# Layer 1 of a two-layer diffusion block: unsplit fp32 expert products for the first 32 blocks, and low parts kept on VectorE up to the expert loop

## Chip, cores and metric

The kernel runs on one core of one Trainium2 chip. The metric is the device time of one execution in microseconds (us), lower is better; for several runs the median is given.

## The reference

Two layers work on 256 latent tokens and 256 context tokens of width 1024. Each layer has an RMSNorm, one input projection, three attention mixers (A, B, W), a gated merge and an output projection; then a second RMSNorm and PEER, a layer of 128 x 128 = 16384 one-neuron experts of which every token picks 16 in each of 8 heads. The last layer computes the latent tokens only.

```python
def peer(h, w_pq, sub_keys, u_tab, v_tab):
    q = (hf @ w_pq).reshape(n, PEER_HEADS, 2, PEER_HALF)
    s = jnp.einsum('nhpd,hpkd->nhpk', q, sub_keys)
    ...
    top_s, pos = lax.top_k(cand_s, PEER_TOPK)
    g = jax.nn.softmax(top_s, axis=-1)
    ...
        a = jax.nn.gelu(jnp.einsum('cd,chkd->chk', hc, u), approximate=False)
        return jnp.einsum('chk,chkd->cd', gc * a, v)
```

For the latent tokens the kernel does not gather the picked experts. It computes all 16384 of them as dense products, 128 blocks of 128 experts, and multiplies each activation by a gate that is zero where the expert was not picked.

## The kernel before

Tokens lie along the free dimension, features along the 128 partitions. A matrix product with a weight comes in two forms.

- **Split** (`wsplit`, `mm3`, `mmw`; lines 292 to 294): a weight tile `raw` of 128 x 1024 is loaded, ScalarE (or VectorE) rounds each half of it to a high part `whi`, VectorE or GpSimd subtracts it to get a low part `wlo`, and TensorE runs three passes: high by high, high by low, low by high. The activation `h` is kept as a high and a low part as well.
- **Unsplit** (`mmd`, line 310): TensorE multiplies the fp32 tile `raw` by an fp32 activation (`h32`). Nothing else touches the weight.

`hmm` chooses between them: unsplit, if it is asked to and an fp32 activation was kept. Only `(layer 0, latent)` is in `DIRECT`, so in layer 1 there is none.

PEER of layer 1 runs in these steps, all recorded in program order by interleaved generators (`weave` gives each a share of the stretch) and then put on five in-order engine queues:

- `topk` (from line 946's scores): 16 query blocks `w_pq`, one product each, then the scores, then the best 16 keys of each half on VectorE (MAX8, FIND_INDEX8, MATCH_REPLACE8).
- `rank`: per 128 tokens the best 16 of 54 candidate pairs and their gates, on VectorE; three transposes on TensorE (line 1034) end it.
- `gbuild`: gate tables `gb` for 32 blocks. Per 16 tokens VectorE makes f16 one-hot tiles `t` (from `iot`), `oh` and `B`, TensorE multiplies them (line 1067, or line 1058 in the packed form of layer 1's loop). `B` has one buffer.
- `up(b)`: the first product of block b (`peer_u`) and its Gelu. Blocks 0 to 31 are computed ahead, in `dense_start`, from 45% of the gate work on, and kept in `gast`.
- `down(b)`: the second product (`peer_v`), in `dense`. In layer 0 (`PLAIN`) it is unsplit (line 1136); in layer 1 the gated activation `mt` is split into `pT` by ScalarE and VectorE, and the weight by `wsplit`. Beside blocks 0 to 31 the table for blocks 32 to 63 is built; from block 30 on `up(b + 2)` stands ahead of `down(b)`.

`lean` is a flag that `wsplit` reads: while it is set, every high part goes to ScalarE and every low part to VectorE. When it is off, `pick` sends each to the engine that its own load count says is free, and some of the low parts go to GpSimd. `norm_mod` and `gated` give some subtractions or additions to GpSimd too when it is off. It is cleared after layer 0's expert loop. Every VectorE, ScalarE and GpSimd instruction is recorded by one helper and shows as line 103.

Of the kernel before, what the change touches and what calls it, by code (L numbers as in the profile page):

```python
# [7 lines left out]
F32 = mybir.dt.float32  # L8
# [9 lines left out]
P = 128  # L18
T = 256
# [10 lines left out]
SW = (32, 32, 32, 32)  # L30
GR = 32
GSCALE = 32768.0
DIRECT = ((0, 0),)
K0, K1, K2 = 0.1, 0.5, 0.06
R0, R1, R2, R3 = 0.6, 0.30, 0.5, 0.9
PACKG = (1,)
# [2 lines left out]
PLAIN = (0,)  # L39
# [8 lines left out]
class Dummy:  # L48
# [5 lines left out]
    def __call__(self, *a, **k):  # L54
        return self

    def __getitem__(self, i):
        return self
# [8 lines left out]
class XView:  # L67


    def __init__(self, tiles):  # L70
        self.tiles = tiles

    def __call__(self, k):
        return self.tiles[k // 4][:, (k % 4) * T:(k % 4 + 1) * T]


class Engine:
# [30 lines left out]
class Net:  # L108
# [63 lines left out]
    def go(self, gen):  # L172
        for _ in gen:
            pass
# [527 lines left out]
    def attend(self, l, g, pre=False):  # L702

        lat = g == 0
        h, q, kv, kvt, f1, ms, ots = self.mx[g]
        kvs = [kv, self.kvc] if lat else [kv]
        m32 = (kvt[:, 0:2048] if lat else f1[:, 4096:6144]).rearrange("p (k t) -> p k t", k=KC)
        att = lambda nm, o: lambda n: n.attention(l, lat, nm, q, kvs, o)
        gq = lambda ch, nm: lambda n: n.gqa_q(l, lat, ch, nm, h, q)
        mb = lambda br, o: lambda n: n.merge_branch(l, br, h, o, m32, ms)  # L710

        def both(f1, f2):
            def run(n):
                yield from f1(n)
                yield from f2(n)
            return run

        if pre:
            yield from self.attention(l, lat, "a", q, kvs, ots[0])
            yield from self.weave(att("b", ots[1]), mb(0, ots[0]))  # L720
        else:
            yield from self.weave(att("a", ots[0]), gq(2, "b"))
            yield from self.weave(att("b", ots[1]), both(gq(3, "w"), mb(0, ots[0])))
        yield from self.weave(att("w", ots[0]), mb(1, ots[1]))
        yield from self.merge_branch(l, 2, h, ots[0], m32, ms)
        gth = self.small(f"gth{g}", [P, KC])
        self.V.tensor_scalar(gth, self.mods[l][:, 16:24, g], 0.5, None, OP.mult)
        xt = self.big.tile([P, 2, 4 * T], F32, tag="tk", name=self.nm("xt"))
        for n in range(2):
            self.nc.sync.dma_start(xt[:, n], self.xd[l, 0, g][n])  # L730
        x = XView([xt[:, n] for n in range(2)])
        ps = [self.psum(True) for _ in range(NTB)]
        for db in range(KC):
            w = self.wsplit(self.d["w_o"][l, db])
            po = self.psum()
            self.mmw(po[:, :T], w, ms[:, 0], ms[:, 1], KC)
            self.defer(lambda po=po, db=db: self.V.scalar_tensor_tensor(x(db), po[:, :T], gth[:, db:db + 1], x(db), OP.mult, OP.add))
            if db:
                self.sumsq(ps, x(db - 1), db - 1)
            yield 2.6  # L740
        self.flush()
        self.sumsq(ps, x(KC - 1), KC - 1)
        for n in range(2):
            self.nc.sync.dma_start(self.xd[l, 1, g][n], xt[:, n])
        htok = None
        if not lat:
            htok = [self.wk.tile([P, D], F32, tag=t, name=self.nm(t)) for t in ("ht", "gacc")]
        h32 = None
        if (l, g) in DIRECT:
            if g:  # L750
                h32 = self.big.tile([P, KC, T], F32, tag="h", bufs=2, name=self.nm("h32"))
            else:
                self.spare = self.gtile()
                h32 = self.spare[:, 0:KC, :]
        self.h32[g] = h32
        self.h2[g] = self.norm_mod(l, g, "g_ffn", 24, x, ps, htok, g == 0 or h32 is None, h32=h32)
        if not lat:
            self.ht = htok[0]
            self.nc.sync.dma_start(self.htok, htok[1])
        yield 1.0  # L760
# [164 lines left out]
    def topk(self, l, g, tok=False):  # L925


        V, S, PE, G = self.V, self.S, self.PE, self.G
        tk = self.big.tile([P, 2048], F32, tag="tk", name=self.nm("tk"))
        r4 = lambda a: a.rearrange("p (h s k) -> p h s k", h=H, s=2)  # L930
        s12 = [r4(tk[:, tb * 256:256 + tb * 256]) for tb in range(NTB)]
        i12 = [r4(tk[:, 512 + tb * 256:768 + tb * 256].bitcast(U32)) for tb in range(NTB)]

        def top16(vals, idx, src, tmp):
            V.max(vals[:, 0:8], src)
            V.max_index(idx[:, 0:8], vals[:, 0:8], src)
            V.match_replace(tmp, vals[:, 0:8], src, -3.0e38)
            V.max(vals[:, 8:16], tmp)
            V.max_index(idx[:, 8:16], vals[:, 8:16], tmp)

        qs = self.work("B", [P, 2, T])

        def score(hb, sk):
            ps = self.psum()
            for tb in range(NTB):
                PE.matmul(ps[:, tb * P:(tb + 1) * P], qs[:, hb % 2, tb * P:(tb + 1) * P], sk, start=True, stop=True)
            sc = self.work("t2", [P, NTB, P])
            S.activation(sc, ps[:, :T].rearrange("p (j e) -> p j e", e=P), AF.Copy)
            for tb in range(NTB):
                tmp = self.work("mt", [P, 256])  # L950
                top16(s12[tb][:, hb // 2, hb % 2, :], i12[tb][:, hb // 2, hb % 2, :], sc[:, tb, :], tmp[:, :P])

        sks = []
        for hb in range(16):
            sks.append(self.work("sk", [P, P]))
            self.nc.sync.dma_start(sks[-1], self.d["subk"][l, hb])
            pq = self.psum()
            self.hmm(pq[:, :T], self.d["w_pq"][l, hb], g)
            self.defer(lambda pq=pq, hb=hb: S.activation(qs[:, hb % 2, :], pq[:, :T], AF.Copy))
            if hb:  # L960
                score(hb - 1, sks.pop(0))
            yield 3.3
        self.flush()
        score(15, sks.pop())
        if tok:
            idx = self.wk.tile([P, NTB, P], U32, tag="gidx", name=self.nm("gidx"))
            gate = self.wk.tile([P, NTB, P], F32, tag="gate", name=self.nm("gate"))
            self.slot[g] = (idx, gate)
        else:
            self.slot[g] = self.big.tile([P, 4, T], F16, tag="slot", name=self.nm("slot"))  # L970
        self.tk = (tk, s12, i12, top16)
# [140 lines left out]
    def dense(self, l):  # L1112
# [12 lines left out]
        def down(b, gb, bi):  # L1125
            if self.late == b:
                self.flush()
            if l in PLAIN:
                w = self.work("pT", [P, T])
                self.mark = V.scalar_tensor_tensor(w, gb[:, bi, :], 1.0 / GSCALE, ga.pop(b), OP.mult, OP.mult)  # L1130
                v = self.load(self.d["peer_v"][l, b], D)
                self.flush()
                for tb in range(NTB):
                    ts = slice(tb * P, (tb + 1) * P)
                    for n in range(2):
                        PE.matmul(acc[tb][n], w[:, ts], v[:, n * 512:(n + 1) * 512], start=b == 0, stop=b == NKEY - 1)  # L1136
                return
            w = self.work("mt", [P, T])
            V.scalar_tensor_tensor(w, gb[:, bi, :], 1.0 / GSCALE, ga.pop(b), OP.mult, OP.mult)
            whl = self.work("pT", [P, 2, T], F32R)  # L1140
            wh, wl = whl[:, 0, :], whl[:, 1, :]
            S.activation(wh, w, AF.Copy)
            V.tensor_tensor(wl, w, wh.bitcast(F32), OP.subtract)
            v = self.wsplit(self.d["peer_v"][l, b])
            for tb in range(NTB):
                ts = slice(tb * P, (tb + 1) * P)
                for n in range(2):
                    self.mm3(acc[tb][n], wh[:, ts], wl[:, ts], v[n][0], v[n][1], b == 0, b == NKEY - 1)
# [127 lines left out]
    def run(self):  # L1276
        self.setup()
        def seq(*fs):
            def run(n):
                for f in fs:  # L1280
                    yield from f(n)
            return run
# [9 lines left out]
        for rate, fs in ((R0, (lambda n: n.weave(seq(f("project", 0, 0), f("attend", 0, 0)),  # L1292
                                                 (seq(f("mod", 0, 5, 6), f("mod", 1, 0, 2)), 0.02, 0.25)),)), (R1, (f("dense_start", 0),)), (R2, (f("dense", 0),))):
            self.go(self.beside(seq(*fs)(self), ctx, rate))
        self.lean = False
        self.go(self.dense_end(0))
        self.go(self.beside(self.project(1, 0, pre=True), ctx, R3))
        go(f("gates0", 1), lambda n: self.rest(n, ctx, f("norm1", 1, 1, True), f("project", 1, 1, kv_only=True)))
        go(f("attend", 1, 0, pre=True), (f("mod_rows", 1, 2, 6, (0,)), 0.0, 0.9))
        self.go(self.dense_start(1))  # L1300
        self.go(self.dense(1))
        self.go(self.dense_end(1))

# [91 lines left out]
```

## Time and profile before

| | |
|---|---|
| median of 3 runs | 3256.76 us (3249.81 to 3266.44) |
| the profiled execution | 3261.69 us, of it span 3259.9 us |
| TensorE matmul busy | 2998.7 us, 92% of the span |
| VectorE busy | 2459.8 us, 75% |
| ScalarE busy | 1259.3 us, 39% |
| GpSimd busy | 1233.5 us, 38%, 550.0 us of it low parts |
| mean granted TensorE clock | 0.956 |

Matmuls are pipelined and their ends are modelled, so a busy TensorE is not yet one at its peak; the time between starts tells its pace. The shares are means over stages with different limits, so the change is read stage by stage. Layer 1 begins at about 1918 us. Its stages are: projections, attention and merge to 2358 us; `topk` to 2421 us; `rank` and the first gate table, with the blocks computed ahead, to 2558.5 us; blocks 0 to 31 of the loop to 2676 us; the other 96 blocks to 3242 us.

### The profile page before, as it was taken

To read this page: it belongs to the slowest core of one execution; us is meant where nothing else is said; L and a number is where in the kernel's file an instruction comes from. 1 tells how busy PE (TensorE), PEld (TensorE's weight loads), DVE (VectorE), ACT (ScalarE), POOL (GpSimd) and SP (SyncE) were. 2 spreads that over 40 slices of the span, in tenths; PEclk is the share of its full clock that TensorE was granted. 3 is DMA by queue.
4 is the path that set the end of the run, shared out by engine and by line. 5 is a ranking of instruction groups with operands and counts; after the bars stand their busy time and mean duration, and the time that the engine had idled before them with its cause. 6 is when DMAs were issued, how large, how long until landed. Compare 5 with 4: busy or idle time off the path is not lost. (4 is left out here: it accounts for less than half of the span.)

```text
span 3259.9 us, 54882 instructions
## 1 busy us (share of the span) xinstructions
PE 2998.7 (92%) x19994; PEld 2443.8 (75%) x19994; DVE 2459.8 (75%) x5282; ACT 1259.3 (39%) x2675; POOL 1233.5 (38%) x959
## 2 busy tenths in 40 slices
PE   8999959888898999999999998999897889999998
PEld 4889835677787646666666666888897769988997
DVE  4767887888899778778887746645578897777665
ACT  4655523444321102222222234444454445555554
POOL 0000023455543254444444424214455565555321
PEclk9999989898999999999999998999998899999999
DMA  7545558788987599999999943524643345555553
GB/s 233 190 137 198 168 180 300 243 293 301 351 314 278 204 331 325 330 328 358 356 351 387 375 141 128 170 94 133 201 154 133 105 138 176 181 177 180 183 187 129
DMA packets 219726, 744.87 MB, mean 228 GB/s; under 512 B 24384, under 2 KB 31936, under 8 KB 219456
## 3 DMA queue, kind: packets, MB, share of 16 engines
q1 hardware_dynamic: 145728, 472.90, 42.6%
q0 software_dynamic: 73728, 268.47, 23.2%
q8 instruction: 157, 2.57, 0.3%
q14 instruction: 113, 0.93, 0.1%
HBM read 735.50 MB, written 5.77 MB: 227 GB/s over the span
## 5 line engine op out<-in xcount | busy, mean ns | idle before, releaser
L103 ACT ACTIVATE whi<-raw 128x512 fp32r<-128x512 f32 (+2 forms) x1137 | 696.2, 622 | 1234.7 <-DMA raw<-peer_u_dram 396.0
L103 POOL TENSOR_TENSOR wlo<-raw,whi 128x512 fp32r<-128x512 f32 (+2 forms) x387 | 550.0, 1434 | 733.0 <-ACT whi L103 490.5
L292 PE MATMUL mm<-h,whi 128*128 128x256 f32 x2624 | 796.3, 304 | 4.1 <-DVE h L103 1.9
L294 PE MATMUL mm<-h,wlo 128*128 128x256 f32 x2624 | 762.4, 291 | 29.5 <-DVE wlo L103 27.3
L293 PE MATMUL mm<-h,whi 128*128 128x256 f32 x2624 | 758.1, 289 | 0.2 <-POOL h L103 0.2
L103 DVE TENSOR_TENSOR wlo<-raw,whi 128x512 fp32r<-128x512 f32 (+1 forms) x823 | 549.8, 682 | 142.9 <-ACT whi L103 139.4
L294 PEld LDWEIGHTS mm<-h,wlo 128*128 128x128 f32 x2624 | 519.2, 198 | 36.3 <-DVE wlo L103 32.9
L292 PEld LDWEIGHTS mm<-h,whi 128*128 128x128 f32 x2624 | 519.3, 198 | 26.6 <-issue 17.4
L293 PEld LDWEIGHTS mm<-h,whi 128*128 128x128 f32 x2624 | 519.5, 198 | 17.3 <-issue 14.3
L103 POOL DMA_INDIRECT ring<-peer_v_dram,gidx x256 | 319.1, 1246 | 399.2 <-DVE gacc L103 282.0
L1136 PE MATMUL acc<-raw,pT 128*128 128x512 f32 x1024 | 460.2, 595 | 1.4 <-DVE pT L103 1.3
L103 POOL DMA_INDIRECT ring<-u_rows_dram,gidx x256 | 315.0, 1231 | 382.8 <-DVE ring L103 285.1
L103 DVE SCALAR_TENSOR_TENSOR gacc<-ring,gaa,gacc 128x1024 f32<-128x1024 f32 x254 | 326.6, 1286 | 75.5 <-DMA ring<-peer_v_dram,gidx 74.1
L103 DVE SCALAR_TENSOR_TENSOR ring<-ring,ht 128x1024 f32<-128x1024 f32 x256 | 307.4, 1221 | 87.9 <-DMA ring<-u_rows_dram,gidx 87.6
L1136 PEld LDWEIGHTS acc<-raw,pT 128*128 128x128 f32 x1024 | 187.2, 191 | 195.0 <-issue 192.6
L294 PE MATMUL acc<-whi,pT 128*128 128x512 f32 x512 | 203.1, 397 | 15.2 <-DVE pT L103 15.2
L103 POOL TENSOR_TENSOR rp_r<-rp_v,mhalf 128x2 f32<-128x2 f32 (+2 forms) x36 | 34.9, 970 | 475.0 <-DVE rp_v L103 473.2
L293 PE MATMUL acc<-wlo,pT 128*128 128x512 f32 x512 | 204.1, 399 | 2.1 <-POOL wlo L103 1.6
L292 PE MATMUL acc<-whi,pT 128*128 128x512 f32 x512 | 205.0, 400 | 0.1
L310 PE MATMUL mm<-gb,raw 128*128 128x256 f32 x768 | 178.0, 389 | 4.0 <-ACT gb L103 4.0
L310 PEld LDWEIGHTS mm<-gb,raw 128*128 128x128 f32 x768 | 147.1, 195 | 24.3 <-ACT gb L103 4.7
L103 DVE TENSOR_TENSOR t<-iot,slot 128x2048 f16<-128x2048 f16 x128 | 163.6, 1278 | 0.2 <-PE mm L1067 0.2
(237 smaller groups left out, 4916.1 us busy)
## 6 DMA issues: line engine op xcount, KB each, us to landing
raw<-peer_u_dram SPq DMA_DIRECT2D x256, 512.0 KB
raw<-peer_v_dram SPq DMA_DIRECT2D x256, 512.0 KB
raw<-w_g_dram SPq DMA_DIRECT2D x72, 512.0 KB
raw<-w_modT_dram SPq DMA_DIRECT2D x56, 512.0 KB
raw<-w_pq_dram SPq DMA_DIRECT2D x48, 512.0 KB
raw<-w_mod_dram SPq DMA_DIRECT2D x40, 512.0 KB
raw<-w_in_dram SPq DMA_DIRECT2D x40, 512.0 KB
raw<-w_br_dram SPq DMA_DIRECT2D x72, 256.0 KB
```

What stands on the lines that cost most here:

```text
L103: return f(*a, **k)
L292: m(out, lh, rh, start=start, stop=False)
L293: m(out, lh, rl, start=False, stop=False)
L294: m(out, ll, rh, start=False, stop=stop)
L310: self.PE.matmul(out, w[:, k * P:(k + 1) * P], r[:, k, :], start=k == 0, stop=k == nk - 1)
L1136: PE.matmul(acc[tb][n], w[:, ts], v[:, n * 512:(n + 1) * 512], start=b == 0, stop=b == NKEY - 1)
```

## The change

Three things, all in layer 1.

- `(1, 0)` joins `DIRECT`: the second norm keeps its fp32 result in two work tiles (`ht`, `gacc`; `HView` makes one index of them), and the 32 blocks computed ahead use it unsplit. `topk` asks for the unsplit form in layer 0 only.
- `down(b)` is unsplit for b < 32.
- `lean` stays set until `dense(1)` begins.

```diff
-DIRECT = ((0, 0),)
+DIRECT = ((0, 0), (1, 0))
...
+class HView:
+    def __init__(self, tiles):
+        self.tiles = tiles
+    def __getitem__(self, i):
+        return self.tiles[i[1] // 4][:, i[1] % 4, i[2]]
...
             if g:
                 h32 = self.big.tile([P, KC, T], F32, tag="h", bufs=2, name=self.nm("h32"))
+            elif l:
+                h32 = HView([self.wk.tile([P, 4, T], F32, tag=t, name=self.nm("h32")) for t in ("ht", "gacc")])
...
-            self.hmm(pq[:, :T], self.d["w_pq"][l, hb], g)
+            self.hmm(pq[:, :T], self.d["w_pq"][l, hb], g, l == 0)
...
-            if l in PLAIN:
+            if l in PLAIN or b < SW[0]:
...
-        self.lean = False
         self.go(self.dense_end(0))
...
         self.go(self.dense_start(1))
+        self.lean = False
         self.go(self.dense(1))
```

Over the whole program TensorE has 768 instructions fewer as the program counts them, ScalarE 116 fewer, GpSimd 241 fewer and VectorE 37 more. GpSimd's low parts fall from 387 to 166; the loads keep their number. The instructions stand in this order. (In the changed file the recording helper is line 113, `mmd` 320, the transposes 1046, the table 1079.)

On VectorE, in the middle of `topk` of layer 1: `tk` holds the chosen values and indices, `t` the scores, `mt` a scratch copy, `wlo` the low half of a query weight. Before:

```order
L103 MAX_INDEX tk_22413<-tk_22413,mt_22886 128x8
L103 MAX tk_22413<-t_4484_22933 128x8 x2
L103 MAX_INDEX tk_22413<-tk_22413,t_4484_22933 128x8
L103 MATCH_REPLACE mt_22935<-tk_22413,t_4484_22933 128x128
L103 MAX_INDEX tk_22413<-tk_22413,t_4484_22933 128x8
L103 MAX tk_22413<-mt_22935 128x8
L103 MATCH_REPLACE mt_22941<-tk_22413,t_4484_22933 128x128
L103 MAX_INDEX tk_22413<-tk_22413,mt_22935 128x8
L103 MAX tk_22413<-mt_22941 128x8
L103 MAX_INDEX tk_22413<-tk_22413,mt_22941 128x8
L103 MAX tk_22413<-t_4495_22988 128x8 x2
```

Of the change:

```order
L113 MAX tk_22407<-t_4412_22597 128x8 x2
L113 MAX_INDEX tk_22407<-tk_22407,t_4412_22597 128x8
L113 MATCH_REPLACE mt_22599<-tk_22407,t_4412_22597 128x128
L113 MAX_INDEX tk_22407<-tk_22407,t_4412_22597 128x8
L113 MAX tk_22407<-mt_22599 128x8
L113 MATCH_REPLACE mt_22605<-tk_22407,t_4412_22597 128x128
L113 MAX_INDEX tk_22407<-tk_22407,mt_22599 128x8
L113 MAX tk_22407<-mt_22605 128x8
L113 TENSOR_TENSOR wlo_22727<-raw_22724,whi_22726 128x512
L113 MAX_INDEX tk_22407<-tk_22407,mt_22605 128x8
L113 TENSOR_TENSOR wlo_22731<-raw_22724,whi_22730 128x512
L113 MAX tk_22407<-t_4423_22652 128x8 x2
```

Most query blocks had both low halves on GpSimd; now both stand on VectorE between two searches, for all 16.

On TensorE, where `rank` of the second 128 tokens ends and the gate table begins: `mm` of three transposes, then the table's first products. Before:

```order
L294 MATMUL mm_24284<-h_22369,wlo_24292 128x256
L292 MATMUL mm_24284<-h_22369,whi_24291 128x256
L293 MATMUL mm_24284<-h_22369,whi_24291 128x256
L294 MATMUL mm_24284<-h_22369,wlo_24292 128x256
L1034 MATMUL mm_24324<-pk,tk_22413 128x128 x3
L1067 LDWEIGHTS t_4724_24331
L1067 MATMUL mm_24338<-B_24335,t_4724_24331 128x32
```

Of the change:

```order
L320 MATMUL mm_23738<-h_4361_22355,raw_23739 128x256 x4
L320 MATMUL mm_23738<-h_4362_22356,raw_23739 128x256 x4
L320 MATMUL mm_23750<-h_4361_22355,raw_23751 128x256 x4
L320 MATMUL mm_23750<-h_4362_22356,raw_23751 128x256 x4
L1046 MATMUL mm_23766<-pk,tk_22407 128x128 x3
L1079 LDWEIGHTS t_4626_23773
L1079 MATMUL mm_23780<-B_23777,t_4626_23773 128x32
```

A block computed ahead was 24 products and is 8 fp32 ones. Between the last scores of `topk` and the first transposes stand 8 such blocks now, 10 more stand ahead of the second ones, and 9 lie between the table's 16 pieces; 5 stand ahead of the last scores.

On VectorE, in blocks 0 to 31 of the loop: `t`, `oh`, `B` and `gb` are the next table, `mt` and `pT` the gated activation. Before:

```order
L103 SCALAR_TENSOR_TENSOR mt_25652<-gb_22412,gast_22410 128x256
L103 TENSOR_TENSOR t_4931_25679<-iot_699,slot_23475 128x2048
L103 TENSOR_TENSOR oh_25681<-iot_699,slot_23475 128x512
L103 TENSOR_TENSOR pT_25627<-mt_25625,pT_25627 128x256
L103 SCALAR_TENSOR_TENSOR mt_25708<-gb_22412,gast_22410 128x256
L103 TENSOR_TENSOR pT_25654<-mt_25652,pT_25654 128x256
L103 TENSOR_TENSOR B_25683<-oh_25681,slot_23475 128x512
L103 TENSOR_TENSOR wlo_25664<-raw_25657,whi_25663 128x512
L103 TENSOR_TENSOR gb_25346<-gb_25346,mm_25603 128x32x8
L103 TENSOR_TENSOR gb_25346<-gb_25346,mm_25614 128x32x8
L103 TENSOR_TENSOR B_25683<-oh_25681,slot_23475 128x512
```

Of the change:

```order
L113 SCALAR_TENSOR_TENSOR pT_24726<-gb_22406,gast_22404 128x256
L113 TENSOR_TENSOR B_24738<-oh_24736,slot_23349 128x512
L113 TENSOR_TENSOR gb_24553<-gb_24553,mm_24696 128x32x8
L113 TENSOR_TENSOR gb_24553<-gb_24553,mm_24707 128x32x8
L113 TENSOR_TENSOR B_24738<-oh_24736,slot_23349 128x512
L113 TENSOR_TENSOR t_4761_24779<-iot_699,slot_23349 128x2048
L113 TENSOR_TENSOR oh_24781<-iot_699,slot_23349 128x512
L113 SCALAR_TENSOR_TENSOR pT_24763<-gb_22406,gast_22404 128x256
L113 SCALAR_TENSOR_TENSOR pT_24771<-gb_22406,gast_22404 128x256
```

A block keeps one VectorE instruction of its own; the low parts of `pT` and of the weight are gone.

## Rows read from the trace of the kernel before

**Rows 1.** Windows by stage: us, busy PE, PEld, DVE, ACT, POOL (count), PEclk, DMA, GB/s.

```profile
1918.50:2358.00 439.50, 397.05 (x2574) 354.71 (x2573) 262.27 (x567) 198.05 (x419) 151.12 (x135) 0.93 0.43 140
2358.00:2421.00 63.00, 62.48 (x526) 62.27 (x525) 44.03 (x250) 35.99 (x77) 38.04 (x30) 1.00 0.55 176
2421.00:2558.50 137.50, 107.35 (x1165) 104.07 (x1163) 119.48 (x311) 57.13 (x109) 68.65 (x44) 0.88 0.35 115
2558.50:2676.00 117.50, 100.19 (x592) 77.19 (x593) 112.18 (x160) 54.09 (x119) 75.57 (x47) 0.93 0.39 126
...
3065.00:3242.00 177.00, 177.00 (x1121) 160.93 (x1121) 113.95 (x159) 96.62 (x187) 41.29 (x32) 1.00 0.54 173
```

**Rows 2.** TensorE's timeline in the late loop: start, us, engine, line, operation, tiles.

```profile
3121.74 0.40 PE L292 MATMUL acc<-whi,pT 128*128 128x512 f32 x1
...
3124.49 0.28 PE L292 MATMUL mm<-h,whi 128*128 128x256 f32 x1
...
3127.36 0.40 PE L292 MATMUL acc<-whi,pT 128*128 128x512 f32 x1
```

**Rows 3.** TensorE's timeline in layer 0, where products are unsplit.

```profile
908.49 3.62 PE L310 MATMUL mm<-gb,raw 128*128 128x256 f32 x16
911.95 0.27 PE L946 MATMUL mm<-sk,B 128*128 128x128 f32 x1
...
1883.12 3.60 PE L1136 MATMUL acc<-raw,pT 128*128 128x512 f32 x8
...
1889.43 1.02 PE L1136 MATMUL acc<-raw,pT 128*128 128x512 f32 x2
```

**Rows 4.** TensorE's timeline: pieces of a gate table, plain and packed.

```profile
2525.32 0.94 PE L1067 MATMUL mm<-B,t 128*128 128x32 f16 x31
2526.11 0.36 PE L292 MATMUL mm<-h,whi 128*128 128x256 f32 x1
...
2696.10 0.65 PE L1058 MATMUL mm<-B,t 128*128 128x64 f16 x16
```

**Rows 5.** Timeline of VectorE and GpSimd while the first table is built.

```profile
2521.20 0.75 DVE L103 TENSOR_TENSOR B<-oh,slot 128x512 f16<-128x512 f16 x2
2523.49 1.64 DVE L103 TENSOR_TENSOR B<-oh,slot 128x512 f16<-128x512 f16 x2
...
2521.66 2.84 POOL L103 TENSOR_TENSOR wlo<-raw,whi 128x512 fp32r<-128x512 f32 x2 [3.60 <-ACT whi L103]
```

**Rows 6.** VectorE's groups, 2421 to 2558.5: busy us, mean ns, idle before.

```profile
L103 DVE TENSOR_TENSOR B<-oh,slot 128x512 f16<-128x512 f16 x34 | 21.9, 680 | 9.1 <-PE mm L1067 8.6
L103 DVE TENSOR_TENSOR t<-iot,slot 128x2048 f16<-128x2048 f16 x17 | 20.6, 1213 | 0.2 <-PE mm L1067 0.2
```

**Rows 7.** VectorE's timeline in `topk`: one search, first and last; two low parts.

```profile
2363.57 0.49 DVE L103 MAX8 tk<-t 128x8 f32<-128x128 f32 x2 [0.70 <-ACT t L103]
...
2365.87 0.29 DVE L103 FIND_INDEX8 tk<-tk,mt 128x8 uint32<-128x128 f32 x1
...
2399.72 0.69 DVE L103 TENSOR_TENSOR wlo<-raw,whi 128x512 fp32r<-128x512 f32 x1
2400.31 0.49 DVE L103 MAX8 tk<-t 128x8 f32<-128x128 f32 x2
```

**Rows 8.** Who waited for whom: us, times, longest. First table, then blocks 0 to 31.

```profile
PE mm L1067 <- DVE B L103: 10.6, 6, 2.0
...
PE mm L1034 <- DVE tk L103: 9.4, 2, 7.3
...
PE acc L294 <- DVE pT L103: 15.2, 7, 2.7
```

**Rows 9.** From 1918.5 to 2358: two waits of TensorE; a VectorE group.

```profile
PE mm L565 <- DVE on L103: 6.9, 2, 4.8
...
PE mm L294 <- DVE wlo L103: 2.8, 1, 2.8
...
L103 DVE SCALAR_TENSOR_TENSOR raw<-raw,cb 128x1024 f32<-128x1024 f32 x32 | 42.7, 1337 | 27.4 <-DMA raw<-w_modT_dram 24.5 <-issue 2.9
```

## The prediction

> **What bounds the kernel now.** I read the busy time by stage first, then TensorE's timeline for what a product costs in each form, then VectorE's groups and timelines, and last the waits. The stages have different limits [rows 1]. In the late loop (3065 to 3242 us) TensorE is busy 177 of 177 us at full clock. In `topk` it is busy 62.5 of 63. In the stretch of `rank` and the first table (2421 to 2558.5) it is busy 107.4 of 137.5 at a clock of 0.88, and VectorE 119.5: VectorE sets the pace. In blocks 0 to 31 VectorE is busy 112.2 of 117.5 and TensorE's clock is 0.93. From 1918.5 to 2358 neither is full (397 and 262 of 439.5): chains from engine to engine hold it. So work taken from VectorE is worth something in the third and fourth stage only, and work added to TensorE costs in the second, and wherever TensorE becomes the bound.
>
> **Price of a product.** Split, a first product takes 3127.36 - 3124.49 = 2.87 us and a second one 3124.49 - 3121.74 = 2.75 us [rows 2]. Unsplit, a first product takes 911.95 - 908.49 = 3.46 us; a second one and a split first one together take 1889.43 - 1883.12 = 6.31 us, so the second one takes 3.44 us [rows 3]. A block thus costs TensorE 0.59 us more in `up` and 0.69 us more in `down`: 41 us for 32 blocks, and it only pays where TensorE waits for the split anyway. The Trainium skill (FP8 and Floating Point Precision, TensorE Precision Notes) says that true fp32 takes four passes through the array; against the split form's three that would be a third more. The rows show 21% and 25%; by the page the extra would be 60 us instead of 41, and the forecast 19 us later. The rows decide.
>
> **Term 1: `topk`, `rank`, first table (2358 to 2558.5, 200.5 us).** TensorE's need after the change: 16 query blocks, still split, at 2.87 us and 0.44 us of scores (an estimate: the 0.27 us of one row [rows 3], four of them, overlapped) = 53.0; 32 blocks ahead at 3.46 = 110.7; the table's 16 pieces of 32 products, at 2526.11 - 2525.32 = 0.79 us [rows 4] = 12.6; transposes about 1.5. Sum 177.8 us. To this come three waits.
>
> First, `topk` turns from TensorE to VectorE. A query block's search lasts 2365.87 + 0.29 - 2363.57 = 2.59 us and its two low parts come 0.59 us apart [rows 7], so 2.59 + 1.18 = 3.77 us on VectorE against 3.31 on TensorE. For the 12 query blocks ahead of the first blocks computed ahead, that is 12 x 0.46 = 5.5 us; after that TensorE has extra products between them and is the longer one.
>
> Second, the 8 blocks between the last scores and the first transposes take 27.7 us. `rank` of the first 128 tokens needs about as long on VectorE, so I take 1 us of wait where the two waits are 9.4 us now [rows 8]. The second `rank` is covered by 10 blocks (34.6 us).
>
> Third, the table. `B` has one buffer, so TensorE waits for it between two pieces with no block between: 10.6 us in 6 waits now, 1.77 each [rows 8]. Those waits hold a pair of `B` that took 1.64 us beside GpSimd's low part, against 0.75 us without it [rows 5]; in the mean 680 ns for one [rows 6], where 0.75 us for two is about 0.4. With GpSimd idle a wait is about 0.85 us; 16 pieces with 9 blocks leave 7 of them, 6.0 us.
>
> Together 177.8 + 5.5 + 1 + 6 = 190.3 us: **10.2 us saved**. Bounds: TensorE's need alone gives 22.7 saved; if all 16 query blocks run at VectorE's pace (7.4) and both present waits stay (9.4 + 10.6), it is 205.2, 4.7 lost.
>
> **Term 2: blocks 0 to 31 (117.5 us).** TensorE's need: 32 x 3.44 = 110.1, the packed table's 16 pieces at 0.65 [rows 4] = 10.4, and the split first products of blocks 32 and 33, 5.7: 126.2 us. VectorE keeps one instruction of about 0.4 us per block, and the table. Per 16 tokens that is `t` 1.2 [rows 6], `oh` and two `B` at 0.4 each, and two additions at 0.4: 3.2 x 16 + 13 = 65 us, half of TensorE's time, so the 15.2 us for which TensorE waits on `pT` [rows 8] go. **8.7 us lost.** Bounds: 5 lost, if the table's pieces pipeline better than 0.65; 15 lost, if half the present waits stay.
>
> **Term 3: `lean` from 1918.5 to 2358.** About 100 low parts move from GpSimd to VectorE and 40 high parts from VectorE to ScalarE: +60 and -24 us on VectorE, which has 177 us idle there. Nothing of the whole stretch hangs on a low part's own length; what is on the path are chains like the 6.9 us for `on` in two waits [rows 9], in which VectorE stood behind GpSimd's low parts. I take the larger of them, 4.8 us, and small change as gained: **5 us saved**. Bounds: 10 saved (that wait and the overlong ones of the modulation rows, whose mean is 1337 ns [rows 9]); 10 lost, the low parts in front of norms and evictions. The norms' subtractions that come back from GpSimd are in this bound.
>
> What is left alone: the 96 later blocks, where TensorE is full and the same instructions run; the DMA queue, whose loads keep number and order and whose engines are busy 0.35 to 0.56 here [rows 1]. The two tiles of `h32` are free by then: the modulation rows' copy ends ahead of the second norm. Their cover gone, they would cost one load's wait, 2 us.
>
> **Sum:** -10.2 + 8.7 - 5 = -6.5 us against the profiled execution (3261.69 us, span 3259.9), which stands 4.9 us above the median of the runs shown. Taken from the median 3256.76: **3250 us**.
>
> **Rivals.** Half a per cent is 16.3 us, about what a measurement of this kernel can tell from no change.
>
> *Faster.* GpSimd's silence is worth more than I take. Many VectorE rows beside a low part are an extra 0.9 us long, and TensorE's clock of 0.88 to 0.93 in three stages comes back once the gaps close. Then term 1 reaches TensorE's need (-22.7), term 2 its low end (+5) and term 3 its gain (-10): -27.7, 3229 us. The Trainium skill (SBUF - State Buffer, Who interferes with whom) states that a VectorE instruction with two SBUF inputs and a GpSimd one that reads SBUF lock each other out for a whole instruction; the pair of 1.64 against 0.75 us agrees, and by that rule this case is the likelier the more of TensorE's waits are locked ones. Against it: term 2 takes TensorE time for certain. Chance 0.27.
>
> *No gain in term 1.* The search, now 3.77 us per query block, runs late throughout, `rank` starts later, and TensorE has its extra 19 us of blocks on top. Term 1 is then 0 and the sum +3.7: 3260 us. For it: `topk` is full on TensorE now, so any wait there is new. Chance 0.19.
>
> *Slower.* Low parts stand behind VectorE's modulation rows. Each of these 32 instructions waits for its load (24.5 us in all, 0.77 each) and lasts 1.34 us [rows 9], and the low parts that GpSimd now makes past them would stand behind them. If every one of the 32 holds TensorE for 2.1 us, less half for the weights already split, that is 33 us instead of -5: 3288 us. It decides from about 20 such holds on. Against it: TensorE waits for a low part in one place of this stretch only (2.8 us [rows 9]), though VectorE makes half of them already. Chance 0.08.
>
> That the change does not do what it says is ruled out nearly wholly by the order of instructions; 0.01 is left for it and the rest.
>
> **Numbers.** The forecast has 0.45, with 3238 to 3264 as its own range. Faster by over 0.5% (under 3240.5): nearly all of the first rival and a sixth of the forecast, 0.33. Slower by over 0.5% (above 3273): the last rival and a rest, 0.09. Within 0.5%: 0.58. The range of 8 in 10 leaves out the slow rival and the far end of the fast one: 3231 to 3266 us.
>
> **What will show it.** Stage by stage in the changed profile: from the first scores to the first `mt` or `pT` of the loop 190 us (178 to 205), with 16 searches some 3.8 us apart at its start; blocks 0 to 31 at 124 to 128 us with TensorE full and at full clock, and VectorE at half; no low part on GpSimd until the loop; the `B` pairs at 0.75 us throughout; the stretch from 1918.5 shorter by some 5 us; the late loop at 5.6 us per block as before. I am wrong if blocks 0 to 31 take no longer than now, if TensorE waits for low parts in the attention stretch, or if `topk` stays at 3.3 us per query block.

## The result and the profile after

The changed kernel takes 3227.02 us (median of 4 runs, 3210.95 to 3230.72), the kernel before 3260.88 in the same series: ratio 0.9892, 95% interval 0.9865 to 0.9918. About 34 us are gained, where 6.5 were forecast. I cut both profiled executions at the same TensorE instructions: the first scores of layer 1's `topk`, the first packed table piece, and a piece of the next table near block 32. Windows by stage of the kernel before, as in [rows 1] but with these cuts: attention stretch; `topk`, `rank` and first table; blocks 0 to 31; the rest.

```profile
1921.20:2358.80 437.60, 395.25 (x2558) 353.09 (x2558) 260.18 (x559) 197.76 (x419) 151.93 (x136) 0.93 0.43 139
2358.80:2558.90 200.10, 169.55 (x1686) 166.27 (x1686) 163.91 (x562) 92.32 (x183) 105.88 (x73) 0.91 0.41 134
2558.90:2696.10 137.20, 119.76 (x724) 94.27 (x725) 129.47 (x184) 64.27 (x139) 87.09 (x54) 0.94 0.41 133
2696.10:3259.90 563.80, 554.40 (x3937) 501.19 (x3936) 384.37 (x652) 295.49 (x603) 229.25 (x159) 0.99 0.54 174
```

And of the changed kernel:

```profile
1926.90:2352.00 425.10, 391.75 (x2559) 349.99 (x2559) 278.82 (x638) 217.67 (x461) 13.31 (x15) 0.94 0.45 143
2352.00:2530.10 178.10, 174.16 (x1430) 158.75 (x1430) 136.15 (x567) 55.06 (x115) 0.00 (x0) 1.00 0.47 145
2530.10:2660.49 130.39, 130.35 (x597) 66.97 (x597) 69.50 (x137) 18.38 (x48) 11.21 (x8) 1.00 0.46 149
2660.49:3225.30 564.81, 555.45 (x3937) 502.34 (x3936) 385.39 (x650) 296.27 (x604) 229.79 (x159) 0.99 0.55 173
```

The stages differ by -12.5, -22.0, -6.8 and +1.0 us; the stretch ahead of them, in which TensorE's instructions are the same and three low parts changed their engine, by +5.7 (1921.2 and 1926.9). In the second and third stage TensorE is now nearly full and at its full clock, where it idled 30.6 and 17.4 us at 0.91 and 0.94. TensorE's waits from 2352 to 2660.5, which answer to [rows 8] (line 1079 was 1067), are gone but for short ones:

```profile
PE mm L1079 <- DVE B L113: 3.1, 6, 0.5
PE mm L1070 <- DVE B L113: 0.9, 1, 0.9
PE mm L958 <- ACT B L113: 0.3, 1, 0.3
```

VectorE's groups from 2352 to 2530, against [rows 6]:

```profile
L113 DVE TENSOR_TENSOR t<-iot,slot 128x2048 f16<-128x2048 f16 x17 | 20.7, 1218 | 0.0
L113 DVE TENSOR_TENSOR wlo<-raw,whi 128x512 fp32r<-128x512 f32 x26 | 17.7, 679 | 0.9 <-ACT whi L113 0.9
L113 DVE TENSOR_TENSOR B<-oh,slot 128x512 f16<-128x512 f16 x34 | 13.0, 421 | 15.1 <-PE mm L1079 15.1
...
L113 DVE TENSOR_TENSOR oh<-iot,slot 128x512 f16<-128x512 f16 x17 | 7.2, 421 | 0.2
...
L113 DVE TENSOR_SCALAR tk<-tk 128x128 f32<-128x128 f32 x12 | 2.5, 222 | 0.0
```

Two of these groups in the kernel before, 2359 to 2558.9:

```profile
L103 DVE TENSOR_TENSOR oh<-iot,slot 128x512 f16<-128x512 f16 x17 | 12.3, 724 | 0.2
...
L103 DVE TENSOR_SCALAR tk<-tk 128x128 f32<-128x128 f32 x12 | 5.7, 488 | 0.0
```

The reader is to see that the same instructions are shorter: `B` fell from 680 to 421 ns, `oh` from 724 to 421, the `tensor_scalar` from 488 to 222. The eight groups of table and `rank` whose mean fell took 76.7 us together before and 50.1 after. `t`, at 1218, did not change. In `topk` one search to the next on VectorE, and one query block's scores to the next on TensorE, against [rows 7]:

```profile
2363.97 0.48 DVE L113 MAX8 tk<-t 128x8 f32<-128x128 f32 x2
...
2366.05 0.67 DVE L113 TENSOR_TENSOR wlo<-raw,whi 128x512 fp32r<-128x512 f32 x1
...
2367.51 0.48 DVE L113 MAX8 tk<-t 128x8 f32<-128x128 f32 x2
```

```profile
2355.39 0.61 PE L958 MATMUL mm<-sk,B 128*128 128x128 f32 x4
2358.71 0.61 PE L958 MATMUL mm<-sk,B 128*128 128x128 f32 x4
```

VectorE needs 3.54 us per query block, TensorE keeps 3.32.

### The profile page after: what moved, and what is told of

It is laid out like the page before. It is cut to its first block, busy times and chain, and to the rows that moved or that the text cites. A ratio compares the mean times of both kernels' runs of the same rounds, so it can differ in the third digit from the quotient of the medians.

```text
span 3225.3 us, 53569 instructions
## 1 busy us (share of the span) xinstructions
PE 3020.4 (94%) x19610; PEld 2411.7 (75%) x19610; DVE 2393.6 (74%) x5319; ACT 1198.2 (37%) x2559; POOL 907.2 (28%) x718
## 5 line engine op out<-in xcount | busy, mean ns | idle before, releaser
L113 ACT ACTIVATE whi<-raw 128x512 fp32r<-128x512 f32 (+2 forms) x1051 | 640.0, 620 | 1133.9 <-DMA raw<-peer_u_dram 401.1
L113 DVE TENSOR_TENSOR wlo<-raw,whi 128x512 fp32r<-128x512 f32 (+2 forms) x916 | 602.3, 671 | 175.7 <-ACT whi L113 169.1
L302 PE MATMUL mm<-h,whi 128*128 128x256 f32 x2368 | 718.3, 304 | 3.0 <-DVE h L113 1.5
L304 PE MATMUL mm<-h,wlo 128*128 128x256 f32 x2368 | 684.2, 289 | 26.6 <-DVE wlo L113 26.4
L303 PE MATMUL mm<-h,whi 128*128 128x256 f32 x2368 | 680.8, 288 | 0.4 <-DVE h L113 0.4
L1148 PE MATMUL acc<-raw,pT 128*128 128x512 f32 x1280 | 574.3, 595 | 1.4 <-DVE pT L113 1.3
L304 PEld LDWEIGHTS mm<-h,wlo 128*128 128x128 f32 x2368 | 464.5, 196 | 32.2 <-DVE wlo L113 31.7
L302 PEld LDWEIGHTS mm<-h,whi 128*128 128x128 f32 x2368 | 464.9, 196 | 23.7 <-issue 15.7
L303 PEld LDWEIGHTS mm<-h,whi 128*128 128x128 f32 x2368 | 465.4, 197 | 18.2 <-issue 14.8
L113 POOL TENSOR_TENSOR wlo<-raw,whi 128x512 fp32r<-128x512 f32 x166 | 240.3, 1463 | 624.0 <-ACT whi L113 451.1
L113 ACT ACTIVATE gb<-mm 128x256 f32<-128x256 f32 (+1 forms) x192 | 84.6, 467 | 255.4 <-PE mm L1079 137.9
L302 PE MATMUL acc<-whi,pT 128*128 128x512 f32 x384 | 150.6, 392 | 0.0
```

The lines of the kernel that those rows point to most:

```text
L113: return f(*a, **k)
L302: m(out, lh, rh, start=start, stop=False)
L303: m(out, lh, rl, start=False, stop=False)
L304: m(out, ll, rh, start=False, stop=stop)
```

## The experiments

**Theory S:** the gain is GpSimd's silence. Its low parts, reading SBUF, delay VectorE's instructions, and TensorE waits for VectorE. **Rival R:** the gain is that unsplit products need no split work, and GpSimd's activity itself costs little. The three parts of the change were run apart and in pairs, then GpSimd's activity by itself, then split products beside a silent GpSimd. In the table stage 2 is `topk` to first table, stage 3 the blocks 0 to 31, cut as above; the ratio is to the kernel before in the same series; TensorE's idle time in the attention stretch is its length less its busy time.

| run | ratio (95% interval) | idle, attention | stage 2 | stage 3 | rest |
|---|---|---|---|---|---|
| before | 1 | 42.4 | 200.1 | 137.2 | 563.8 |
| changed | 0.9892 (0.9865 to 0.9918) | 33.4 | 178.1 | 130.4 | 564.8 |
| e1 | 0.9952 (0.993 to 0.9973) | 33.5 | 182.3 | 140.8 | 563.8 |
| e2 | 0.9934 (0.991 to 0.9958) | 40.2 | 180.8 | 136.1 | 563.3 |
| e3 | 0.9919 (0.9893 to 0.9946) | 33.6 | 179.6 | 136.8 | 563.2 |
| e4 | 0.991 (0.9882 to 0.9938) | 39.6 | 178.2 | 130.4 | 564.7 |
| e5 | 0.9939 (0.9911 to 0.9966) | 34.6 | 188.6 | 130.4 | 563.0 |
| e6 | 0.9914 (0.9874 to 0.9953) | 31.8 | 178.3 | 130.3 | 563.0 |
| e7 | 0.99 (0.9868 to 0.9931) | 33.7 | 178.2 | 119.7 | 565.6 |
| e8 | 0.989 (0.9852 to 0.9927) | 34.3 | 175.6 | 119.5 | 563.8 |
| e9 | 0.9866 (0.9822 to 0.9909) | 33.7 | 178.5 | 116.7 | 565.8 |
| e10 | 0.9864 (0.983 to 0.9898) | 34.4 | 178.3 | 113.8 | 564.1 |
| e11 | 0.9898 (0.9864 to 0.9933) | 34.3 | 178.2 | 130.3 | 563.6 |
| e12 | 0.9863 (0.982 to 0.9906) | 34.6 | 178.2 | 119.8 | 563.9 |
| e13 | 0.991 (0.9892 to 0.9928) | 34.4 | 185.3 | 117.7 | 564.2 |
| e14 | 0.987 (0.9849 to 0.9891) | 34.9 | 178.8 | 110.2 | 563.8 |

Where TensorE bounds stages 2 and 3 and the program is the same, they repeat within half a us; the whole does not, since the place of the first scores lies anywhere from 2342.9 to 2366.5 us. In e13 and e14 the second product of block 0 stands ahead of the first packed piece (12 and 8 matmuls more in stage 2), so that their two stages compare with the others' only as a sum.

**e1: only the third part.** Against the kernel before:

```diff
-        self.lean = False
         self.go(self.dense_end(0))
...
         self.go(self.dense_start(1))
+        self.lean = False
         self.go(self.dense(1))
```

> Only the third part of the change: the low parts stay on VectorE up to the expert loop, every product split as before. Theory S (GpSimd's silence pays): the stretch up to the first scores keeps its 12.5 us; in topk, rank and the first table VectorE has about 96 low parts at 0.59 us (57 us) beside some 118 us of other work, 175 us, against 159 us of TensorE, so that the stage lasts about 180 us instead of 200; the blocks stay at 134. In all about 30 us less than before, ratio 0.990. Theory R (what pays is that the unsplit products have no split work, silence counts for little): VectorE, loaded with 30 us more in that stage, is the bound at over 200 us there; in all -12 to +5 us, ratio 0.996 to 1.002.

Its windows of stages 2 and 3, and the longest of TensorE's waits in stage 2:

```profile
2357.30:2539.60 182.30, 164.45 (x1687) 161.80 (x1688) 176.46 (x631) 93.29 (x183) 10.16 (x4) 0.94 0.45 145
2539.60:2680.41 140.81, 120.00 (x725) 93.74 (x725) 134.46 (x184) 64.32 (x139) 87.04 (x55) 0.94 0.41 132
```

```profile
PE mm L304 <- DVE wlo L113: 10.2, 3, 4.4
```

Stage 2 takes 182.3 us with every product split, and VectorE is busy 176 of them: theory S's number, not R's. The ratio is short of the 0.990 expected: the blocks lasted 3.6 us more than before, at a TensorE that idled 20.8 us of them. That VectorE carried a backlog into them is argued, not shown (e13 comes back to it).

**e2: only the first part.** The changed kernel with `lean` cleared where it was, and

```diff
-            if l in PLAIN or b < SW[0]:
+            if l in PLAIN:
```

> Only the first part: the 32 first products ahead are unsplit, low parts shared with GpSimd as before, second products split. Theory S: topk still has some 11 low parts on GpSimd, but rank and the table run beside a silent GpSimd, 180 us instead of 200; nothing elsewhere; about -20 us, ratio 0.994. Theory R: the same -20 us. A third view, that the three parts only work together: 0 us.

Stage 2 took 180.8 us, as both theories had it; in that stage the first part does not need the other two.

**e3: without the second part** (e2's diff alone).

> The change without its second part (second products of blocks 0 to 31 split again, low parts shared with GpSimd there). If the unsplit second products gain the 6.8 us that the stage shows, this kernel takes about 7 us longer than the changed one, about 28 us less than before, ratio 0.991. If the 6.8 us come from VectorE entering the loop without a backlog, it is as fast as the changed one or up to 10 us faster (TensorE's own need is 22 us less).

Stage 3 takes 136.8 us, 6.4 more than in the changed kernel. TensorE has 13.0 us less to do there (117.4 against 130.4), but idles 19.4 us. Most of that idle time is the wait of [rows 8] for `pT` again:

```profile
2546.10:2682.89 136.79, 117.37 (x725) 91.75 (x725) 132.02 (x185) 64.28 (x139) 86.06 (x53) 0.96 0.42 132
...
PE acc L304 <- DVE pT L113: 17.0, 10, 2.7
```

So the first reading holds: with GpSimd at work, unsplit second products gain 6 to 7 us.

**e4: without the third part** (`lean` cleared where it was).

> The change without its third part: low parts are shared with GpSimd from the end of layer 0's loop on, as before. If the 12.5 us of the stretch up to the first scores are what moving the low parts is worth, this kernel takes about 12 us longer than the changed one, ratio to before 0.993; the stage from the first scores to the first packed piece stays within 180 us, since 32 low parts of topk are all that is left to share. If the stretch's gain is run to run, it equals the changed kernel.

Stage 2 is within bounds. TensorE's idle time in the attention stretch is 39.6 us instead of 33.4: of the 12.5 us about half is the third part's, not all.

**e5 and e6: work for GpSimd that nothing needs.** e5, in `ups`; e6 has `self.nc.gpsimd.memset(self.nz, 0.0)` in place of the last line:

```diff
                     self.up(l, b, self.ga[b], True)
+                    if l and b > 1:
+                        self.nc.scalar.activation(self.nz, self.ga[b - 2], AF.Copy)
+                        for _ in range(3):
+                            self.nc.gpsimd.tensor_tensor(self.nz, self.nz, self.nz, OP.subtract)
```

> The changed kernel with work for GpSimd that nothing needs: behind each of the blocks 2 to 31 ahead ScalarE copies the activation of two blocks before into a scratch tile and GpSimd makes three subtractions of that tile from itself (90 instructions of 128x256 that read and write SBUF, about 0.75 us each by the rows of h, 68 us of the 130 in which rank and the first table run). No low part moves. Theory S (what GpSimd's low parts cost was VectorE's time, instruction by instruction): VectorE's B instructions go from a mean of 421 ns to 550 to 700, oh from 421 likewise, the B waits of TensorE come back, the stage from the first scores to the first packed piece goes from 178 to 184 to 195 us. Theory R (the low parts cost because TensorE waited for GpSimd's own results): B stays at 421 ns, the stage at 178 to 180 us.

> As the run with GpSimd's reads, but GpSimd fills the scratch tile with zeros three times instead: 90 instructions that write SBUF and read none. If any activity of GpSimd delays VectorE, B lengthens as in the run with reads, in proportion to GpSimd's busy time. If it is only its reads, B stays at 421 to 450 ns and the stage at 178 to 181 us.

Stage 2 of e5, with VectorE's and GpSimd's groups and TensorE's waits there:

```profile
2345.10:2533.70 188.60, 179.14 (x1430) 161.17 (x1431) 157.82 (x567) 65.54 (x145) 77.75 (x90) 0.98 0.43 137
```

```profile
L113 DVE TENSOR_TENSOR B<-oh,slot 128x512 f16<-128x512 f16 x34 | 18.3, 575 | 8.5 <-PE mm L1080 8.5
...
L1118 POOL TENSOR_TENSOR nz<-nz 128x256 f32<-128x256 f32 x90 | 77.7, 864 | 113.5 <-ACT nz L1116 108.8
...
PE mm L1047 <- DVE tk L113: 4.6, 1, 4.6
PE mm L1080 <- DVE B L113: 3.7, 7, 1.0
```

And the groups of e6:

```profile
L113 DVE TENSOR_TENSOR B<-oh,slot 128x512 f16<-128x512 f16 x34 | 12.9, 419 | 15.1 <-PE mm L1080 15.1
...
L1118 POOL MEMSET nz<- 128x256 f32 x90 | 28.3, 315 | 151.0 <-ACT nz L1116 147.5
```

Reads whose results no product needs cost 10.5 us of stage 2: `B` is 575 ns long, VectorE's busy time rises from 136 to 158 us for the same 567 instructions, and TensorE's wait for `rank` is back. Writes cost 0.2 us and `B` is unchanged. In proportion to GpSimd's busy time `B` should have been 421 + 154 x 28.3 / 77.7 = 477 ns, so it is the reads. ScalarE's copies do wait for GpSimd in e5 (36.9 us, 0.9 in e6), but that is not what TensorE loses: its waits for ScalarE are 0.3 us, as in the changed kernel, and VectorE's waits for ScalarE are no longer than in e6. Rival R falls: in e5 no low part moved. The other theory of e5's expectation, that TensorE waited for GpSimd's own low parts, had this for it in stages 2 and 3 of the kernel before, 3.5 us in all:

```profile
PE mm L294 <- POOL wlo L103: 1.9, 2, 1.7
...
PE acc L293 <- POOL wlo L103: 1.6, 4, 0.5
```

**e7 to e10: split products beside a silent GpSimd.** All four clear `lean` at block 32 instead of ahead of the loop. e7 (e10 has `b % 4 == 0`, e9 no second condition at all):

```diff
-            if l in PLAIN or b < SW[0]:
+            if l in PLAIN or b < SW[0] and b % 2:
...
             def run(n):
+                if l == L - 1 and i == 1 and n is not n.cnt:
+                    self.lean = False
...
-        self.lean = False
         self.go(self.dense(1))
```

e8 adds, for the first products ahead:

```diff
-                    self.up(l, b, self.ga[b], True)
+                    self.up(l, b, self.ga[b], l == 0 or b < 4 or b % 2 == 0)
```

> The changed kernel with every second of the second products of blocks 0 to 31 split again, and all low parts on VectorE until block 31 is done. TensorE saves 16 x 0.69 = 11 us; VectorE gets 16 x 1.6 = 26 us on top of 68 in 128. If that stage is bound by TensorE alone, it goes from 130 us to about 120 and the kernel takes 10 us less than the changed one (3217, ratio 0.986). If VectorE's chains (table, then second factor, then low parts) become the bound, it stays at 128 to 134.

> As the run with half of the second products, and every second of the first products ahead from block 5 on split too (14 products, 14 x 0.59 = 8 us less for TensorE, 14 x 1.18 = 17 us more for VectorE, which is busy 136 of 178). If TensorE alone bounds that stage, 178 goes to 170 and the kernel is 18 us ahead of the changed one (ratio 0.984). If VectorE's table bounds its end, the B waits grow and the stage stays at 176 to 182.

> The changed kernel with all second products of blocks 0 to 31 split again, but no low part on GpSimd until block 31 is done. In the kernels with these products split and GpSimd at work the blocks last 136 to 141 us. TensorE needs 130.4 - 32 x 0.69 = 108 us; VectorE has 69.5 us of the changed kernel and 32 x 1.6 = 51 more, 121 us. If GpSimd's silence is what matters in the blocks too, they last 121 to 126 us, less than the 130.4 of the unsplit ones, and the kernel is 5 to 9 us ahead of the changed one. If the blocks were slow because of the split work itself, they stay at 134 to 141.

> Second products of blocks 0 to 31 unsplit in every fourth block only, silent GpSimd until block 31 is done. TensorE needs 130.4 - 24 x 0.69 = 114 us, VectorE 69.5 + 24 x 1.6 = 108 us. If the two stay apart as well as with one in two (119.7 measured, 119.4 by the same sum), the stage lasts 114 to 116 us. If VectorE's bursts for the table make TensorE wait, 118 to 124.

Stage 3 of e7, e9 and e10 (one fence each), then stage 2 of e8:

```profile
2526.70:2646.43 119.73, 119.60 (x661) 77.57 (x661) 89.28 (x183) 39.72 (x92) 8.29 (x6) 1.00 0.45 153
```

```profile
2524.90:2641.61 116.71, 112.07 (x724) 88.43 (x724) 113.50 (x228) 65.05 (x140) 8.96 (x6) 1.00 0.50 155
```

```profile
2523.70:2637.50 113.80, 113.79 (x692) 83.95 (x693) 103.72 (x207) 53.02 (x116) 9.02 (x6) 1.00 0.50 160
```

```profile
2362.70:2538.30 175.60, 166.21 (x1542) 156.68 (x1543) 154.68 (x600) 73.18 (x148) 0.00 (x0) 1.00 0.47 153
```

e9 is the plainest test: every second product split again, 116.7 us against 136.8 in e3, and less than the 130.4 of the unsplit ones. VectorE makes all the low parts there and is busy 113.5 us (228 instructions); before, with GpSimd's help, it was busy 129.5 (184). e7 and e10 land on TensorE's sum (119.4 and 114). By the ratio of the whole e7 is level with the changed kernel (0.99 and 0.9892), where 0.986 was expected; only its stage shows the gain. e8 misses: TensorE's busy time falls by 8.0 us as worked out, but 5.4 come back, as a wait for `rank` of 3.4 and longer `B` waits (4.5 instead of 3.1), and its ratio is 0.989 instead of 0.984.

**e11 and e12: GpSimd silent to the end.** e11 is the changed kernel without the line that clears `lean`; e12 is e7 without the two lines that clear it.

> The changed kernel with no low part on GpSimd in the later 96 blocks either. VectorE, busy 385 of the last 565 us, loses the delays that GpSimd causes it and gets 159 low parts at 0.59 us, 94 us; ScalarE, busy 296, gets the high parts that VectorE makes now. TensorE idles 9 us there. If TensorE is the bound, at most 9 us are gained: 556 to 565. If VectorE's and ScalarE's chains become late (479 and some 400 of 565), the stretch grows to 570 or more.

> The run with half of the second products unsplit, and no low part on GpSimd to the end. If both effects stand by themselves: blocks 119.7 us, the last stretch as in the run with GpSimd silent to the end, in all 10 us less than that run.

The last stretch of e11, and two groups of VectorE in it, then the same groups of the changed kernel:

```profile
2659.93:3223.50 563.57, 553.59 (x3937) 500.34 (x3936) 410.59 (x777) 312.29 (x635) 0.70 (x1) 0.99 0.56 173
```

```profile
L113 DVE TENSOR_TENSOR wlo<-raw,whi 128x512 fp32r<-128x512 f32 x374 | 257.3, 691 | 142.6 <-ACT whi L113 138.5
L113 DVE TENSOR_TENSOR pT<-mt,pT 128x256 fp32r<-128x256 f32 x94 | 39.4, 419 | 0.0
```

```profile
L113 DVE TENSOR_TENSOR pT<-mt,pT 128x256 fp32r<-128x256 f32 x94 | 69.2, 736 | 11.0 <-ACT pT L113 11.0
L113 DVE CAST whi<-raw 128x512 fp32r<-128x512 f32 x31 | 47.0, 1517 | 44.0 <-PE acc L304 39.9 <-POOL wlo L113 4.0
```

Little or nothing is gained there (563.6 and 564.8): TensorE is busy 554 of the 564 us, and VectorE's relief buys nothing. VectorE is busy 411 us, not the 479 I worked out, for its other instructions became shorter (`pT` from 736 to 419 ns). e12 is e11 and e7 added up.

**e13 and e14: no product unsplit, and a mixture.** e13 is e9 with layer 1 taken out of `DIRECT` again: the kernel before, with a silent GpSimd to block 31. e14 is e10 with e8's second diff.

> The kernel before with one thing changed: no low part on GpSimd until block 31 is done; every product split as before. If GpSimd's low parts cost all that the change gains, this kernel has the 182 us of the run with low parts alone from the first scores to the first packed piece, and the 116.7 us of the run with split second products in the blocks: 299 us against 308.5 of the changed kernel and 337 before; 10 us less than the changed kernel, ratio 0.987. If unsplit products are needed, so that VectorE comes into the blocks without a backlog, the blocks last 121 us or more and the kernel is level with the changed one.

> The quickest parts of the runs together: every second first product ahead split from block 5 on (175.6 us measured from the first scores to the first packed piece), second products unsplit in every fourth block (113.8 us), GpSimd silent until block 31 is done. If the two stages stand by themselves, 289.4 us against 308.5 of the changed kernel: 19 us less, ratio 0.984. If the split first products hand VectorE's backlog on to the blocks, 116 us or more there.

Stages 2 and 3 of e13:

```profile
2354.20:2539.50 185.30, 168.81 (x1699) 164.88 (x1699) 178.78 (x641) 94.67 (x186) 0.00 (x0) 0.94 0.46 147
2539.50:2657.23 117.73, 110.37 (x714) 86.14 (x713) 108.00 (x225) 63.48 (x137) 11.36 (x6) 1.00 0.48 150
```

e13's two stages take 303.0 us, a little more than the 299 expected and 5.5 less than the changed kernel's 308.5; by its ratio it is level with the changed kernel. No product had to be unsplit. The 4.0 us beyond the sum are about what e1's blocks took too long, which fits a backlog of VectorE, but no run takes the two apart. e14 takes 289.0 us (289.4 expected), the least of all; the two stages add up. By their ratios e9, e10, e12 and e14 cannot be told apart (0.986 to 0.987). All four lie ahead of the changed kernel's 0.9892, but the intervals overlap and the series differ, so that the whole times alone do not show it; the shorter stages do.

## Why the prediction was wrong

The sign was right and the time was not: 3250 forecast, 3227 measured, outside of the range, and 2 us from the first rival's 3229. That rival's mechanism, GpSimd's silence, is what e5, e6, e9 and e13 show.

**Term 2 failed, by sign.** "Blocks 0 to 31 (117.5 us)" took the wrong length for the stage before. I had ended it where VectorE takes up block 31, while TensorE was behind. The last row of VectorE's timeline for that block, and TensorE's first instruction of block 32's second product, in the kernel before:

```profile
2674.99 1.52 DVE L103 SCALAR_TENSOR_TENSOR mt<-gb,gast 128x256 f32<-128x256 f32 x1
```

```profile
2693.35 0.40 PE L292 MATMUL acc<-whi,pT 128*128 128x512 f32 x1
```

The same place in the changed kernel, whose stage begins at 2530.10:

```profile
2657.74 0.40 PE L302 MATMUL acc<-whi,pT 128*128 128x512 f32 x1
```

From 2558.9 to 2693.35 it is 134.4 us. The split first product of block 34 (2.87) lies in that stretch too; with it the 126.2 us worked out for the change are 129.1, a gain of 5 and no loss. The new length was nearly right: to the same place it is 127.6 us. That the blocks took less time than before was one of the signs of being wrong. A stage has to be cut at one engine's instructions, the bound's. And though the price of unsplitting was right (32 x 0.69 = 22 us), the choice was not between unsplit products and the waits of before: e9 shows the third way, split and silent, 13.7 us below.

**Term 1 was sized 12 us too small.** The stage took 178.1 us, not 190.3. TensorE's need, 177.8 us in the sum, was 174.2 us busy: the stage begins at the first scores, and only 14 of the 16 query products lie behind them (112 matmuls of line 302, 8 each), 5.7 us less; that 177.8 lies next to the measured 178.1 is luck. The three waits on top, 12.5 us in the sum, came to 3.9 us of idle time. *`topk` becomes VectorE-bound*, 5.5 us: VectorE does need more than TensorE, but 3.54 us and not 3.77, in part since the rows' durations overlap by some 0.1 us from one instruction to the next and I added a whole search; and its lag of 0.22 us per query block costs nothing: no wait for `wlo` in that stage. "If `topk` stays at 3.3 us per query block" I called a sign of error, and it did. *`rank`*, 1 us: none. *`B`*, 6.0 us: 3.1 in 6 waits and one of 0.9. All three were worked out with VectorE's rows as they were beside GpSimd's reads, with one correction for `B`; the seven other groups (17.7 of the 26.6 us by which the eight fell) I left as they were.

**Term 3 had the right place, in part.** Forecast -5, and TensorE's idle time in the attention stretch fell by about 7 us: 31.8 to 34.9 us in the thirteen profiles that keep the low parts on VectorE, 39.6 to 42.4 in the three that don't. Of the wait in [rows 9], 6.9 us with a longest of 4.8, this is left, so that it gave 2.9 us and not 4.8; the wait for `wlo` gave another 2.4:

```profile
PE mm L575 <- DVE on L113: 4.0, 2, 2.5
```

Of the 12.5 us between the two profiles 9.0 are idle time and 3.5 TensorE's busy time there, 395 and 392 us for the same products. The busy time ran from 388 to 402 us over all profiles, at granted clocks of 0.95 to 0.91, whatever the kernel.

**The rivals.** No gain in term 1 is out. The slower one, low parts behind the modulation rows, did not come: 0.4 us of waits on `wlo` in the stretch. The first had the right cause at 0.27 and missed in term 2, which it still booked as a loss of 5; its term 1 came out (-22.7 and -22.0) and its term 3 nearly (-10 and -12.5). That its 3229 us lies 2 us from the result is in part luck: its terms add up to 27.7 us where 34 were measured, and they are taken from a median of 3256.76, where the kernel before had 3260.88 in the series of the result.

## What to carry to other kernels

Before shifting work to a half-idle GpSimd, price what its reads do to VectorE: in blocks 0 to 31 VectorE with all the low parts (e9) was busy for less time than VectorE with GpSimd's help, and TensorE waited less; in stage 2 (e1) VectorE was busy longer, 176 us against 164, and the stage was shorter all the same. When an instruction's mean differs between two stages of one profile, take the undisturbed one for the forecast, for every group and not just for the one that is looked at. Cut stages at the instructions of the engine that will be the bound, or its backlog is booked as somebody else's time.

## What the runs showed of the hardware

GpSimd's reads of SBUF lengthen some of VectorE's instructions and not others. Beside low parts or e5's subtractions `B` went from 421 to 575 and 680 ns and `oh` from 421 to 565 and 724, and the `tensor_scalar`, which has one input, from 222 to 427 and 488; the casts of 128x512 in the late loop lasted 1517 ns in the mean, the shortest of the 31 532. The searches kept their means (MATCH_REPLACE8 282 and 281 ns). e6's writes left `B` at 419 and `oh` at 420, though the `tensor_scalar` rose to 269. The Trainium skill (SBUF — State Buffer, Who interferes with whom) says that a VectorE instruction with two SBUF inputs contends with GpSimd instructions that read SBUF and not with those that only write it. e5 and e6 agree, in `B` and `oh`. `t`, which has two SBUF inputs as well, kept its mean in stage 2 (1213 ns before, 1218 in the changed kernel), but not everywhere. Here are stage 2 of e5, stage 3 of e3 with GpSimd at work, and stage 3 of e7 with GpSimd silent:

```profile
L113 DVE TENSOR_TENSOR t<-iot,slot 128x2048 f16<-128x2048 f16 x17 | 24.4, 1434 | 0.0
```

```profile
L113 DVE TENSOR_TENSOR t<-iot,slot 128x2048 f16<-128x2048 f16 x17 | 29.4, 1726 | 0.0
```

```profile
L113 DVE TENSOR_TENSOR t<-iot,slot 128x2048 f16<-128x2048 f16 x17 | 20.6, 1215 | 0.0
```

Why it kept its mean in stage 2 of the kernel before, no run here tells.

The granted clock went with TensorE's gaps. Its two levels are 1.2 and 2.4 GHz; 1.00 stands for the upper one throughout, and a mean below it holds stretches at the lower. In stage 2 it was 1.00 where TensorE idled 4 us (changed kernel) and 9.4 us (e8), 0.98 at 9.5 us (e5), 0.94 at 17.9 us (e1), 0.91 at 30.6 us (before). So a wait that goes can give back busy time too: in stage 3, with the same products, TensorE was busy 117.4 us at 0.96 in e3 and 112.1 at 1.00 in e9, so that of the 20.1 us between them 5.3 are busy time and 14.8 idle time. In the attention stretch, where TensorE has gaps in every kernel, the clock lay between 0.91 and 0.95. That, and the first mark's place between 1912.7 and 1931.7 us, ahead of which TensorE's instructions are the same in all the kernels, go with a spread of 20 us between runs of one kernel (3210.95 to 3230.72 for the changed one), against which stages are the sharper measure.
